# The sink attention's products with v, two token blocks at a time

## The chip, the cores and the metric

The kernel runs on one core of one Trainium2 chip. The metric is the device time of one execution in microseconds (us), as the median of several runs. TensorE is called PE here, VectorE DVE, ScalarE ACT, GpSimd POOL and SyncE SP; PEld is TensorE's loading of weights, which runs beside its products.

## What is computed

The reference is a trunk of two layers (`DEPTH = 2`) over 512 tokens of width 1024. In each layer three token mixers run side by side on the same normalised input: a neighbourhood attention, a sliding-window attention with a sink, and a bidirectional gated DeltaNet. Their outputs are projected, gated and summed; then come an output projection and a gated MLP with a convolution. The change touches the second mixer alone, which has 8 query heads and 2 key/value heads of 64 and works in blocks of 128 tokens. A query block sees its own block of keys and the neighbour on either side:

```python
def sliding_window_gqa(q, k, v, sink):
    ...
    s = jnp.einsum('bnqhgd,bnkhd->bnhgqk', qb, kb).astype(jnp.float32) * (HEAD_DIM ** -0.5)
    ...
    s = jnp.where(valid[None, :, None, None], s, -jnp.inf)
    ...
    p = jax.nn.softmax(jnp.concatenate([s, sink_col], axis=-1), axis=-1)[..., :-1].astype(v.dtype)
    return jnp.einsum('bnhgqk,bnkhd->bnqhgd', p, vb).reshape(B, L, Hq, d)
```

There are four blocks, so the first and the last have two key blocks and the two in the middle three.

## The kernel before

Activations lie with their features on the partitions and all 512 tokens in the free dimension. Every dense product takes 128 x 128 weights and 512 tokens and is made of three PE products (lines 152 to 154: high by high, high by low, low by high part). Weights are loaded by SP's queue (line 140), and split into a high part on ACT (line 142) and a low part on DVE or POOL (line 144).

The source lists the steps of a layer in the order `sp np gg na gp sa gx gz gs gm gc go mn ms mg`: projections, the two attentions (`na`, `sa`), the DeltaNet's parts (`gx`: cross products, `gs`: solve, `gm`: mid, `gc`: scan, `go`: output) and the three merges (`mn`, `ms`, `mg`). That order gives priorities only. A scheduler lays out each engine's stream from all steps at once (`schedule_with_timeline_sim=True`), with times that it plans itself, and packs the buffers in SBUF and PSUM (`auto_bufs=True`); the numbers in `NB` and `CAPS` say how many buffers a name has. Within an engine, instructions then run in the order laid out. `tc.issue_after(x)` puts instructions of a block behind `x` in the stream of x's engine.

`swa_attend` (step `sa`) has two passes (`ep`), each over four token blocks (`b`), each with four heads at a time (two of `e`, two of `gq`). In a block PE makes the scores into banks `at` (lines 529 and 530), DVE adds the mask, scales them and takes the extreme (line 533), ACT takes the exponential (line 541) and scales by the reciprocal sum (line 545). Then for each key block PE transposes the four heads' probabilities into one bank (line 553), and ACT copies it to an SBUF tile `th` (line 555, recorded as line 80, the helper `copy`). Behind the block's last transpose stand the products with v (line 560): each key block gives two products of the source and four PE instructions in the trace, 64 columns of weights wide, for the column halves of the array. They sum into `py`, a bank of `at` that is taken at line 546. ACT writes the high part of `py` to `ysh` (line 564), DVE the low part to `ysl` (line 565). `ms` multiplies both by the branch weights.

`na_attend` (step `na`) has a like inner loop with its products at line 456; it collects the transposed probabilities of two token blocks in a list `pend` and runs the products of both behind the second block's last transpose (line 446).

Of the kernel before, what the change touches and what calls it, by code (L numbers as in the profile page):

```python
# [7 lines left out]
F32 = mybir.dt.float32  # L8
# [3 lines left out]
AF = mybir.ActivationFunctionType  # L12
ALU = mybir.AluOpType
# [34 lines left out]
CAPS = {n + i: c for n, c in (("nqs", 2), ("nkh", 2), ("y", 4), ("ma", 4), ("mg", 8), ("gt", 2), ("W", 2),  # L48
                              ("qd", 2), ("wn", 2), ("vs", 1), ("z", 1), ("act", 22)) for i in "01"}
# [1 line left out]
ORDER = "np na sp sa gg gp gx gs gm gc gz go mn ms mg"  # L51
MERGE = "nsg"
NB = {"mm": 4, "gd": 3, "at": 4, "raw": 3, "hi": 3, "lo": 3}
CAPS |= {}
NB |= {"mm": 6, "gd": 3, "at": 5, "raw": 3, "hi": 3, "lo": 3}
ORDER = "sp np gg na gp sa gx gz gs gm gc go mn ms mg"
MERGE = "nsg"
# [4 lines left out]
def encoder_kernel(ctx, tc, xT, wall, par, cst, nab, out, depth=2, dbg=None):  # L62
    nc = tc.nc
    V, S, T, G = nc.vector, nc.scalar, nc.tensor, nc.gpsimd
# [13 lines left out]
    def copy(name, out, in_, e="S"):  # L78
        if ENG.get(name, e) == "S":
            return S.activation(out=out, in_=in_, func=AF.Copy)  # L80
        return V.tensor_copy(out, in_)
# [3 lines left out]
    def nm(s):  # L85
        cnt[0] += 1
        return f"{s}_{cnt[0]}"
# [4 lines left out]
    def big(dt=F32, shape=(128, 1024), name="u", ln=None):  # L92
        ln = ln or line[0]
        return up.tile(list(shape), dt, tag="u_" + name, name=nm(name), bufs=CAPS.get(name, 1))
# [4 lines left out]
    def tmp(dt=F32, shape=(128, 512), name="t", ln=None):  # L99
        ln = ln or line[0]  # L100
        key = name if name in CAPS else (ln or line[0]) + "_" + name
        return tp.tile(list(shape), dt, tag=key, name=nm(name), bufs=CAPS.get(key, 3))

    def bank(tag, shape=(128, 512)):
        return ps.tile(list(shape), F32, tag=tag, name=nm(tag), bufs=NB[tag])
# [12 lines left out]
    def small(n, name, bufs=3):  # L118
        turn[name, n] = turn.get((name, n), -1) + 1
        return kept(f"{name}{n}_{turn[name, n] % bufs}", n)  # L120
# [165 lines left out]
    for l in range(depth):  # L286
# [224 lines left out]
        def swa_attend():  # L511
            line[0] = "a"

            y["s"] = [None] * 4
            for ep in range(2):
                yh, yl = (big(F32R, (128, 2, 512), name=n) for n in ("ysh", "ysl"))
                for e in range(2):
                    y["s"][2 * ep + e] = (yh[:, e], yl[:, e])
                for b in range(4):
                    kb0, kb1 = max(0, b - 1), min(4, b + 2)  # L520
                    w = 128 * (kb1 - kb0)
                    pr_ = [None] * 4
                    for e in range(2):
                        c0 = 8 * b + 4 * ep + 2 * e
                        mx, sk = small(2, "s", 8), slice(4 * ep + 2 * e, 4 * ep + 2 * e + 2)
                        for gq in range(2):
                            sc = bank("at")
                            q_, kc = qs[2 * ep + e][gq][:, 128 * b:128 * b + 128], slice(128 * kb0, 128 * kb1)
                            T.matmul(sc[:, 0:w], lhsT=q_, rhs=kdh[gq][:, kc], start=True, stop=False)  # L529
                            T.matmul(sc[:, 0:w], lhsT=q_, rhs=kdl[gq][:, kc], start=False, stop=True)  # L530

                            pr = tmp(name="spr")
                            V.tensor_tensor_reduce(out=pr[:, 0:w], in0=sc[:, 0:w], in1=smask[:, 128 * (b == 0):128 * (b == 0) + w], scale=rqs[:, c0 + gq:c0 + gq + 1],
                                                   scalar=nsink[:, sk.start + gq:sk.start + gq + 1], op0=ALU.add, op1=ALU.min, accum_out=mx[:, gq:gq + 1])
                            pr_[2 * gq + e] = pr
                        es, rs = small(2, "s", 8), small(2, "s", 8)
                        V.tensor_tensor(es, mx, P[:, P_SK + sk.start:P_SK + sk.stop], op=ALU.add)
                        S.activation(out=es, in_=es, func=AF.Exp)
                        for gq in range(2):
                            pr = pr_[2 * gq + e]  # L540
                            S.activation(out=pr[:, 0:w], in_=pr[:, 0:w], func=AF.Exp, bias=mx[:, gq:gq + 1], scale=-1.0, accum_out=rs[:, gq:gq + 1])
                        V.tensor_tensor(rs, rs, es, op=ALU.add)
                        V.reciprocal(rs, rs)
                        for gq in range(2):
                            S.activation(out=pr_[2 * gq + e][:, 0:w], in_=pr_[2 * gq + e][:, 0:w], func=AF.Copy, scale=rs[:, gq:gq + 1])
                    py = bank("at")

                    pTs = []
                    for kb in range(kb0, kb1):
                        pt = bank("at")  # L550
                        c0 = 128 * (kb - kb0)
                        for i in range(4):
                            lt = T.transpose(pt[:, 128 * i:128 * i + 128], pr_[i][:, c0:c0 + 128], ident)  # L553
                        pT = tmp(name="th")
                        copy("th", pT, pt)
                        pTs.append(pT)
                    with tc.issue_after(lt.ins):
                        for kb, pT in zip(range(kb0, kb1), pTs):
                            for gq in range(2):
                                T.matmul(py[64 * gq:64 * gq + 64, 0:256], lhsT=vst[:, 128 * kb + 64 * gq:128 * kb + 64 * gq + 64],  # L560
                                         rhs=pT[:, 256 * gq:256 * gq + 256], start=kb == kb0, stop=kb == kb1 - 1, tile_position=(0, 64 * gq))
                    bs = slice(128 * b, 128 * b + 128)
                    pyv = py[:, 0:256].rearrange("p (e t) -> p e t", e=2)
                    S.activation(out=yh[:, :, bs], in_=pyv, func=AF.Copy)
                    V.tensor_tensor(yl[:, :, bs], pyv, yh.bitcast(F32)[:, :, bs], op=ALU.subtract)

        def gdn_gates():
            line[0] = "g"
# [352 lines left out]
        def merge(i, bn):  # L921
# [14 lines left out]
            for m0 in range(0, 8, 2):  # L936
# [6 lines left out]
                for q in range(2):  # L943
# [12 lines left out]
                    elif i == 2:  # L956
# [4 lines left out]
                        mg.append((mh, ml))  # L961

        steps = {"np": na_project, "na": na_attend, "sp": swa_project, "sa": swa_attend, "gg": gdn_gates, "gp": gdn_project,
                 "gx": gdn_cross, "gs": gdn_solve, "gm": gdn_mid, "gc": gdn_scan, "gz": gdn_z, "go": gdn_out}
        for i in ORDER.split():
# [19 lines left out]
        for i in range(NFF):  # L985
            cv = []
            for c in range(2):
# [3 lines left out]
                t = tmp(name="cv", ln=ln)  # L991
# [182 lines left out]
```

## Time and profile before

| | us |
|---|---|
| median of 3 runs | 1661.05 |
| lowest and highest of them | 1659.44 and 1661.3 |
| the profiled execution | 1657.82 |
| its span, first to last instruction | 1656.0 |
| PE busy in the span | 1626.6 |
| DVE, ACT, POOL busy | 1009.8, 767.0, 530.1 |

The profile is of one execution, 3.2 us below the median of the runs. Its span leaves out 1.8 us around the program. Busy time of PE counts the modelled length of its pipelined products, of which the next one starts before the last has ended; how fast PE goes is read from starts that follow each other.

### The profile page before, as it was taken

To read this page: it belongs to the slowest core of one execution; us is meant where nothing else is said; L and a number is where in the kernel's file an instruction comes from. 1 tells how busy PE (TensorE), PEld (TensorE's weight loads), DVE (VectorE), ACT (ScalarE), POOL (GpSimd) and SP (SyncE) were. 2 spreads that over 40 slices of the span, in tenths; PEclk is the share of its full clock that TensorE was granted. 3 is DMA by queue.
4 is the path that set the end of the run, shared out by engine and by line. 5 is a ranking of instruction groups with operands and counts; after the bars stand their busy time and mean duration, and the time that the engine had idled before them with its cause. 6 is when DMAs were issued, how large, how long until landed. Compare 5 with 4: busy or idle time off the path is not lost.

```text
span 1656.0 us, 25095 instructions
## 1 busy us (share of the span) xinstructions
PE 1626.6 (98%) x9196; PEld 1300.2 (79%) x9196; DVE 1009.8 (61%) x1907; ACT 767.0 (46%) x1500; POOL 530.1 (32%) x512
## 2 busy tenths in 40 slices
PE   7999999998999999999999999999999999999999
PEld 5777787676888888878887777876788888888887
DVE  5699895454747777741137998855566577777200
ACT  5556666522444444443335665664234444444321
POOL 0333210130035554554406231102200455455543
PEclk9999999999999999999999999999999999999999
DMA  6222221121532323244333222111225322223442
GB/s 211 87 80 74 86 74 37 33 93 54 184 122 90 99 93 100 95 128 137 125 107 103 80 69 77 52 39 40 89 88 180 115 95 95 99 95 110 134 134 73
DMA packets 91499, 160.45 MB, mean 97 GB/s; under 512 B 10352, under 2 KB 17136, under 8 KB 91376
## 3 DMA queue, kind: packets, MB, share of 16 engines
q1 hardware_dynamic: 91376, 158.85, 29.7%
q8 instruction: 72, 1.18, 0.3%
q14 instruction: 51, 0.42, 0.1%
HBM read 147.80 MB, written 8.39 MB: 94 GB/s over the span
## 4 chain that ended last, share of the span: by engine, by line
PE 85%; DVE 5%; issue 4%; POOL 3%; ACT 2%; DMA 1%; SPq 0%; POOLq 0%; DVEq 0%; ACTq 0%
PE mm L152 24%; PE mm L154 24%; PE mm L153 24%; POOL wl L144 2%; PE at L560 1%; PE at L553 1%; DVE wl L144 1%; PE gd L710 1%; PE at L529 1%; PE at L456 1%; PE gd L843 1%; PE at L530 1%; PE gd L875 1%; PE gd L825 1%; PE gd L346 0%
## 5 line engine op out<-in xcount | busy, mean ns | idle before, releaser
L152 PE MATMUL mm<-hh,wh 128*128 128x512 f32 x1408 | 557.5, 396 | 11.2 <-ACT wh L142 9.9
L154 PE MATMUL mm<-hh,wl 128*128 128x512 f32 x1408 | 555.9, 395 | 5.2 <-DVE wl L144 5.1
L153 PE MATMUL mm<-hl,wh 128*128 128x512 f32 x1408 | 554.9, 395 | 0.5 <-DVE hl L222 0.5
L144 POOL TENSOR_TENSOR wl<-wr,wh 128x512 fp32r<-128x512 f32 (+1 forms) x272 | 363.3, 1347 | 556.7 <-ACT wh L142 545.3
L142 ACT ACTIVATE wh<-wr 128x512 fp32r<-128x512 f32 (+1 forms) x512 | 312.5, 617 | 328.1 <-PE mm L153 222.1
L152 PEld LDWEIGHTS mm<-hh,wh 128*128 128x128 f32 x1408 | 265.9, 189 | 71.5 <-ACT wh L142 12.4
L154 PEld LDWEIGHTS mm<-hh,wl 128*128 128x128 f32 x1408 | 265.9, 189 | 66.0 <-DVE wl L144 9.2
L153 PEld LDWEIGHTS mm<-hl,wh 128*128 128x128 f32 x1408 | 265.8, 189 | 59.0 <-DVE hl L222 3.0
L144 DVE TENSOR_TENSOR wl<-wr,wh 128x512 fp32r<-128x512 f32 x240 | 174.8, 731 | 97.9 <-ACT wh L142 93.5
L245 DVE SCALAR_TENSOR_TENSOR cv<-up,fix,cv 128x511 f32<-128x511 f32 x88 | 143.1, 1626 | 2.8
L154 PE MATMUL mm<-act,wl 128*128 128x512 f32 x352 | 137.1, 390 | 0.6 <-POOL wl L144 0.6
L244 DVE SCALAR_TENSOR_TENSOR cv<-up,fix,cv 128x511 f32<-128x511 f32 x88 | 83.0, 945 | 89.7 <-ACT cv L243 89.7
L152 PE MATMUL mm<-act,wh 128*128 128x512 f32 x352 | 137.1, 389 | 0.3 <-ACT wh L142 0.3
L153 PE MATMUL mm<-act,wh 128*128 128x512 f32 x352 | 137.0, 389 | 0.0
L243 ACT ACTIVATE cv<-up,fix 128x512 f32<-128x512 f32 x88 | 70.8, 809 | 35.5 <-DVE up L291 35.5
L166 ACT ACTIVATE act<-cv 128x512 fp32r<-128x512 f32 x44 | 27.8, 632 | 126.9 <-DVE cv L995 126.9
L154 PEld LDWEIGHTS mm<-act,wl 128*128 128x128 f32 x352 | 66.1, 188 | 15.3 <-POOL wl L144 1.2
L152 PEld LDWEIGHTS mm<-act,wh 128*128 128x128 f32 x352 | 66.1, 188 | 14.2 <-ACT wh L142 0.7
L153 PEld LDWEIGHTS mm<-act,wh 128*128 128x128 f32 x352 | 66.1, 188 | 13.7
L872 POOL TENSOR_TENSOR sd<-SA,fix 64x256 f32<-64x256 f32 x24 | 15.5, 646 | 177.5 <-DVE SA L882 135.5
L1013 DVE TENSOR_TENSOR xo<-xo,mm 128x512 f32<-128x512 f32 x8 | 5.5, 688 | 105.1 <-PE mm L154 105.1
L994 ACT ACTIVATE cv<-cv 128x512 f32<-128x512 f32 x44 | 27.8, 632 | 83.8 <-DVE cv L245 83.8
(292 smaller groups left out, 2153.1 us busy)
## 6 DMA issues: line engine op xcount, KB each, us to landing
wr<-in_wall_dram SPq DMA_DIRECT2D x496, 256.0 KB, 2.8
xs<-xo SPq DMA_DIRECT2D x16, 256.0 KB, 2.2
xo<-xs SPq DMA_DIRECT2D x16, 256.0 KB, 3.9
sw<-raw SPq DMA_DIRECT2D x40, 64.0 KB, 2.0
xf<-in_xT_dram SPq DMA_DIRECT2D x8, 256.0 KB, 6.2
xo<-in_xT_dram SPq DMA_DIRECT2D x8, 256.0 KB, 3.4
xf<-xs SPq DMA_DIRECT2D x8, 256.0 KB, 3.8
wr<-in_wall_dram SPq DMA_DIRECT2D x16, 128.0 KB, 3.1
```

The source lines that it names most:

```text
L142: S.activation(out=hi[:, :n], in_=raw[:, :n], func=AF.Copy)
L144: (G if c >= CH_UP else V).tensor_tensor(lo[:, :n], raw[:, :n], hi.bitcast(F32)[:, :n], op=ALU.subtract)
L152: T.matmul(acc, lhsT=wh, rhs=rh, start=start, stop=False)
L153: T.matmul(acc, lhsT=wh, rhs=rl, start=False, stop=False)
L154: lastm[0] = T.matmul(acc, lhsT=wl, rhs=rh, start=False, stop=stop)
L166: S.activation(out=hi, in_=src, func=AF.Copy)
L243: S.activation(out=dst, in_=src, func=AF.Identity, scale=w[:, 1:2], bias=bias)
L244: V.scalar_tensor_tensor(dst[:, 1:L], src[:, 0:L - 1], w[:, 0:1], dst[:, 1:L], op0=ALU.mult, op1=ALU.add)
L245: V.scalar_tensor_tensor(dst[:, 0:L - 1], src[:, 1:L], w[:, 2:3], dst[:, 0:L - 1], op0=ALU.mult, op1=ALU.add)
L456: T.matmul(py[64 * e:64 * e + 64, 128 * b_:128 * b_ + 128], lhsT=(vt[j][0:wi, b_ + i] if b_ + i < 4 else vt4[0:wi, j])[:, 64 * e:64 * e + 64],
L529: T.matmul(sc[:, 0:w], lhsT=q_, rhs=kdh[gq][:, kc], start=True, stop=False)
L994: S.activation(out=cv[0], in_=cv[0], func=AF.Silu)
```

## The change

In `swa_attend` the list `pend` now lives over the four blocks of a pass. An even block makes its scores, probabilities, transposes and copies as before, puts its key blocks on the list, and goes on. An odd block does the same, then takes the bank `py`, now with a place for either block, and runs the products of both blocks behind its own last transpose. One ACT and one DVE instruction then evict both blocks' columns, 512 instead of 256. The bank is taken behind the transposes instead of ahead of them. `th` in this step gets five buffers where it had three.

```diff
--- before.py
+++ after.py
@@ -51,7 +51,7 @@
 ORDER = "np na sp sa gg gp gx gs gm gc gz go mn ms mg"
 MERGE = "nsg"
 NB = {"mm": 4, "gd": 3, "at": 4, "raw": 3, "hi": 3, "lo": 3}
-CAPS |= {}
+CAPS |= {"a_th": 5}
 NB |= {"mm": 6, "gd": 3, "at": 5, "raw": 3, "hi": 3, "lo": 3}
 ORDER = "sp np gg na gp sa gx gz gs gm gc go mn ms mg"
 MERGE = "nsg"
@@ -516,6 +516,7 @@
                 yh, yl = (big(F32R, (128, 2, 512), name=n) for n in ("ysh", "ysl"))
                 for e in range(2):
                     y["s"][2 * ep + e] = (yh[:, e], yl[:, e])
+                pend = []
                 for b in range(4):
                     kb0, kb1 = max(0, b - 1), min(4, b + 2)
                     w = 128 * (kb1 - kb0)
@@ -543,9 +544,7 @@
                         V.reciprocal(rs, rs)
                         for gq in range(2):
                             S.activation(out=pr_[2 * gq + e][:, 0:w], in_=pr_[2 * gq + e][:, 0:w], func=AF.Copy, scale=rs[:, gq:gq + 1])
-                    py = bank("at")
-
-                    pTs = []
+
                     for kb in range(kb0, kb1):
                         pt = bank("at")
                         c0 = 128 * (kb - kb0)
@@ -553,16 +552,21 @@
                             lt = T.transpose(pt[:, 128 * i:128 * i + 128], pr_[i][:, c0:c0 + 128], ident)
                         pT = tmp(name="th")
                         copy("th", pT, pt)
-                        pTs.append(pT)
+                        pend.append((b, kb, pT, kb == kb0, kb == kb1 - 1))
+                    if b % 2 == 0:
+                        continue
+                    py = bank("at", (128, 2, 2, 128))
                     with tc.issue_after(lt.ins):
-                        for kb, pT in zip(range(kb0, kb1), pTs):
+                        for b_, kb, pT, st, sp_ in pend:
                             for gq in range(2):
-                                T.matmul(py[64 * gq:64 * gq + 64, 0:256], lhsT=vst[:, 128 * kb + 64 * gq:128 * kb + 64 * gq + 64],
-                                         rhs=pT[:, 256 * gq:256 * gq + 256], start=kb == kb0, stop=kb == kb1 - 1, tile_position=(0, 64 * gq))
-                    bs = slice(128 * b, 128 * b + 128)
-                    pyv = py[:, 0:256].rearrange("p (e t) -> p e t", e=2)
-                    S.activation(out=yh[:, :, bs], in_=pyv, func=AF.Copy)
-                    V.tensor_tensor(yl[:, :, bs], pyv, yh.bitcast(F32)[:, :, bs], op=ALU.subtract)
+                                T.matmul(py[64 * gq:64 * gq + 64, b_ % 2], lhsT=vst[:, 128 * kb + 64 * gq:128 * kb + 64 * gq + 64],
+                                         rhs=pT[:, 256 * gq:256 * gq + 256], start=st, stop=sp_, tile_position=(0, 64 * gq))
+                    pend = []
+                    bs = slice(128 * b - 128, 128 * b + 128)
+                    pyv = py.rearrange("p b e t -> p e b t")
+                    S.activation(out=yh[:, :, bs].rearrange("p e (b t) -> p e b t", b=2), in_=pyv, func=AF.Copy)
+                    V.tensor_tensor(yl[:, :, bs].rearrange("p e (b t) -> p e b t", b=2), pyv,
+                                    yh.bitcast(F32)[:, :, bs].rearrange("p e (b t) -> p e b t", b=2), op=ALU.subtract)
 
         def gdn_gates():
             line[0] = "g"
```

## Rows read from the trace of the kernel before

**Rows 1.** The page: busy time of the engines, and the chain that ended last.
```profile
PE 1626.6 (98%) x9196; PEld 1300.2 (79%) x9196; DVE 1009.8 (61%) x1907; ACT 767.0 (46%) x1500; POOL 530.1 (32%) x512
...
PE 85%; DVE 5%; issue 4%; POOL 3%; ACT 2%; DMA 1%; SPq 0%; POOLq 0%; DVEq 0%; ACTq 0%
```

**Rows 2.** Busy us by stretch: PE, PEld, DVE, ACT, POOL; then clock, DMA share, GB/s.
```profile
199.00:326.00 127.00, 125.51 (x1162) 96.73 (x1160) 86.44 (x236) 81.25 (x200) 12.20 (x22) 0.99 0.16 51
...
1017.00:1152.00 135.00, 133.87 (x1216) 101.32 (x1214) 90.08 (x243) 81.96 (x202) 12.49 (x22) 0.99 0.15 48
```

**Rows 3.** PE in order of time (start us, us) at two visits of line 560.
```profile
215.41 0.39 PE L152 MATMUL mm<-hh,wh 128*128 128x512 f32 x1
215.64 0.39 PE L153 MATMUL mm<-hl,wh 128*128 128x512 f32 x1
215.96 0.65 PE L560 MATMUL at<-th,sv 128*64 128x256 f32 x4
216.54 0.44 PE L529 MATMUL at<-kdh,qs 128*128 128x384 f32 x1
...
1036.07 1.08 PE L560 MATMUL at<-th,sv 128*64 128x256 f32 x8
1037.09 0.45 PE L529 MATMUL at<-kdh,qs 128*128 128x384 f32 x1
```

**Rows 4.** Line 560's PE busy time in the eight even blocks' stretches.
```profile
215.00:219.00 4.00, 1.30 (x8) 1.00 0.44 134
...
314.00:318.00 4.00, 1.96 (x12) 1.00 0.10 26
1036.00:1039.00 3.00, 1.08 (x8) 1.00 0.12 46
...
sum 32.00, PE 12.61; mean PE 1.58
```

**Rows 5.** The same in the eight odd blocks' stretches.
```profile
235.00:238.00 3.00, 1.52 (x12) 1.00 0.00 0
...
sum 31.00, PE 11.94; mean PE 1.49
```

**Rows 6.** Groups of instructions (count | busy us, mean ns | idle before).
```profile
L80 ACT ACTIVATE th<-at 128x512 f32<-128x512 f32 x40 | 21.2, 595 | 19.0 <-PE at L553 18.9
...
L565 DVE TENSOR_TENSOR ysl<-at,ysh 128x256 fp32r<-128x256 f32 x16 | 6.7, 420 | 0.7 <-ACT ysh L564 0.6
...
L564 ACT ACTIVATE ysh<-at 128x256 fp32r<-128x256 f32 x16 | 6.1, 380 | 10.7 <-PE at L560 10.7
...
L815 DVE TENSOR_TENSOR kE<-gd,fix 128x512 f32<-128x512 f32 x8 | 5.5, 684 | 0.1
```

**Rows 7.** PE in order of time at a pair of the neighbourhood attention.
```profile
953.96 0.27 PE L446 MATMUL at<-fix,lg 128*120 128x128 f32 x1
954.16 0.81 PE L456 MATMUL at<-pT,nvt 64*64 64x128 f32 x8
...
958.80 0.66 PE L456 MATMUL at<-pT,nvt 128*64 128x128 f32 x8
```

**Rows 8.** ACT at three copies, and PE at a late copy, in order of time.
```profile
296.55 1.57 ACT L80 ACTIVATE th<-at 128x512 f32<-128x512 f32 x3 [1.18 <-PE at L553]
...
1150.10 0.65 PE L560 MATMUL at<-th,sv 128*64 128x256 f32 x4 [0.58 <-ACT th L80]
1150.68 0.68 PE L863 MATMUL gd<-SA,wn 64*64 64x64 f32 x16
```

**Rows 9.** PE in order of time, behind the scan in layer 0.
```profile
388.95 0.66 PE L205 MATMUL gd<-fix,rb 128*128 128x128 f32 x4 [2.61 <-DVE rb L201]
```

**Rows 10.** PE in order of time, then the two stretches of lower clock.
```profile
242.87 3.79 PE L779 MATMUL gd<-WT,Xo 32*32 32x32 f32 x126
...
247.49:250.91 3.41, 3.41 (x10) 0.50 0.30 82
...
1063.28:1066.69 3.41, 3.41 (x9) 0.50 0.23 77
```


## Prediction

> **What bounds the kernel now.** I read the page first, for the share of the engines and the chain that ended last: TensorE (PE) is busy 98% of the span and carries 85% of the chain, the rest being split over engines with 5% or less [rows 1]. Then the table by stretches for the two places where the sink attention runs, one in each layer: of 127.0 us PE is busy 125.5 in the first and of 135.0 us 133.9 in the second, while ScalarE (ACT) and VectorE (DVE) are busy some two thirds [rows 2]. So PE has work at nearly every moment there: dense products, the gated DeltaNet's and the attention's lie mixed in one stream. What the change takes out of ACT or DVE is worth nothing directly; what it takes out of PE's stream moves everything behind it up. What it could gain by ending waits is bounded by PE's idle time in both stretches, (127.0 - 125.5) + (135.0 - 133.9) = 2.6 us.
>
> Then PE's order of time around line 560, the product with v. These products are 64 columns of weights wide, and almost everything around them is 128 wide. I call a run of them with nothing else between a visit. One key block gives four PE instructions. A plain dense product starts 0.23 us after the one before it; the first product of a visit starts 0.32 us after a dense one, a visit of four takes 0.58 us until the next instruction starts, one of eight takes 1.02 us [rows 3]. So four more products inside a visit cost 0.44 us, but a visit of four by itself lengthens PE's stream by 0.32 + 0.58 - 0.23 = 0.67 us. The difference, 0.67 - 0.44 = 0.23 us, is the price of going there and back, whatever is done there.
>
> How many visits there are I read from the same products in sixteen stretches, one for each token block in each of four passes (two ep in two layers). A stretch with eight products is busy 1.08 us if they are one visit and 2 x 0.65 = 1.30 us if they are two; one with twelve is busy 1.96 us in three visits [rows 4]. So each visit shows 0.65 us for its first four products and 0.43 us for every further four. The even blocks (b = 0 and 2) have 80 products, 20 fours, busy 12.61 us in all: 20 x 0.43 = 8.6 us, and (12.61 - 8.6) / 0.22 = 18 visits [rows 4]. The odd blocks have the other 20 fours in 11.94 us: (11.94 - 8.6) / 0.22 = 15 visits, one of them with all twelve products of its block [rows 5]. So there are 33 visits for 16 blocks, because a block's key blocks mostly come apart.
>
> **The change, part by part.**
>
> *Products.* It removes none: 160 stay. It takes away the even block's own place: its products wait for the last transposes of the odd block, some 15 to 20 us later (the first block's run in the stretch from 215, the second's in that from 235 [rows 4, 5]). By then the copies of the even block's two or three key blocks are long made, so they can issue as one visit: 8 first visits for 8 pairs. What comes with them of the odd block is the open quantity. Its key blocks have been transposed just before, and ACT copies them one after another at 0.60 us each [rows 6]; those not ready at that moment make visits of their own. Two bounds and an extreme: none joins, 8 + 15 = 23 visits; the first odd visit always joins, 15; everything joins, 8. The savings against 33 are 10, 18 and 25 visits, at 0.23 us: 2.3, 4.1 and 5.8 us. The nearest rows for the choice are those of the neighbourhood attention, which already runs its products by pairs of blocks: the eight of the even block start right behind the last transposes, those of the odd block 4.6 us later, each a visit of its own [rows 7]. That speaks for the upper count; but there the odd block has one copy step, here two or three, and the first is made while the others are transposed. I take the middle, 19 visits: 14 x 0.23 = 3.2 us saved.
>
> Here a rule can be weighed. The row's 0.23 us per visit stands by itself [rows 3]. The Trainium skill, "TensorEngine Tiling (Array Packing)", Key Properties, says that changing the tiling mode drains TensorE; the trace agrees that there is a price for it, though it names none. Taken with the source's loop, where a block is one run, it would count 16 changes before and 8 after, and the sum would be 8 x 0.23 = 1.8 us; by the visits that the trace shows it is 3.2.
>
> *Evictions.* 16 of 256 columns become 8 of 512: on ACT 16 x 0.380 = 6.1 us become 8 x 0.595 = 4.8, by the copy of 512 columns from PSUM; on DVE 16 x 0.420 = 6.7 become 8 x 0.684 = 5.5, by the nearest row of 512 columns out of PSUM [rows 6]. The 2.5 us are on engines with a third of their time free [rows 2]: nothing. The last eviction before the merge is longer, 0.595 + 0.684 - 0.380 - 0.420 = 0.48 us; PE hides it with merge products that read the other heads' results and with gate products. With no cover it costs 0.48 us at four places, 1.9 us; I take none.
>
> *The bank.* Line 546 takes a PSUM bank for the products ahead of the transposes, in each block; the new code takes one behind the transposes of two blocks. An even block then holds none, and the odd block's scores have a rival fewer for the `at` banks. That can only end waits of PE, so it is between nothing and the 2.6 us of idle time above; I take nothing, since ready dense work fills PE already.
>
> *The transposed probabilities.* Five buffers instead of three, so that five key blocks can be held. No instruction and no DMA more; no queue of SP or POOL is passed.
>
> *What is queued behind the new wait.* The products stand in PE's own order. If the last copy is late when they issue, all PE work behind them waits, the scan's products too. Before, that happened once worth naming: 0.58 us at 1149.5, behind a copy, with the scan's next products queued behind it [rows 8].
>
> Sum against the profiled execution (1657.8 us, span 1656.0): 1657.8 - 3.2 = 1654.6. The median of the runs shown is 3.2 us above that execution, so the forecast for the median is 1661.05 - 3.2 = 1657.8, or 0.2% faster.
>
> **Rivals.**
>
> *All products join.* One visit a pair, 8 in all, and some of PE's idle 2.6 us as well: 5.8 to 8.4 us saved, about 1655 to 1652.6. For it: an even block with eight products and an odd one with twelve already issue in one run [rows 4, 5]. Against: the neighbourhood attention's pairs [rows 7], and that 15 visits for eight odd blocks are nearly two for each.
>
> *It hardly does what it says.* Key blocks of the even blocks go on coming apart, since the scheduler places products by its own planned times and slips dense work between them as it does now; or what is saved at 200 to 330 is lost at PE's waits later in the layer. One such wait of 2.61 us stands at 386, behind the DeltaNet's output norm on DVE, with no other work for PE [rows 9]: if that norm comes no sooner, layer 0 gives back its half. Half of 3.2 stays: 1.6 us, about 1659.5, no change that can be measured. (About 0.2%, 3.3 us, is what can be told from no change.)
>
> *Slower: PE waits for the copies.* If all five key blocks' products are placed right behind the last transposes, PE stands until the odd block's copies are done, up to 1.57 us for three [rows 8]. Eight times that is 12.6 us, less the 5.8 us that single visits save: 6.8 us slower, about 1668. It decides from (5.8 + 3.3) / 8 = 1.1 us a pair. Against: PE carried this wait once in 33 visits, since elsewhere other work was put in between.
>
> *Slower: the clock.* The granted clock fell to 0.50 of full (1.2 of 2.4 GHz) twice, for 3.41 us, the first time right after 126 tiny products of line 779; in those 3.41 us PE had 10 and 9 products where 15 fit at 0.23 us, so a fall costs at least 5 x 0.23 = 1.2 us [rows 10]. If twenty narrow products behind forty transposes did the same, it would be slower by over 0.2% from (3.2 + 3.3) / 1.2 = 5.4, six of the eight pairs; all eight give 9.6 - 3.2 = 6.4 us slower, about 1667. The rows speak against it: the visit of twelve, behind twelve transposes, kept the full clock [rows 5]. In a sentence apart: the Trainium skill, "TensorE: Matmul & The Clock Gate", Part 4, says that a transpose on TensorE does not count as busy for the clock in the same way, which would put longer runs of transposes and narrow products at risk.
>
> *The order elsewhere.* All engines' orders come from one plan over the whole program, and buffers share memory; one edit can move waits far away. Such waits are of 0.5 to 2.6 us each; a handful more or fewer gives 4 us either way.
>
> **How the numbers follow.** Forecast (15 to 23 visits, the rest as it is: 2.3 to 4.1 us saved) 0.50, half of it beyond 3.3 us; all join 0.12; hardly anything 0.12; waiting for copies 0.07; clock 0.03; order elsewhere 0.16 (faster 0.08, same 0.02, slower 0.06). Faster: 0.25 + 0.12 + 0.08 = 0.45. Same: 0.25 + 0.12 + 0.02 = 0.39. Slower: 0.07 + 0.03 + 0.06 = 0.16. The forecast's own range is 1657.0 to 1658.8. The range given is 1652.5, where all join and the idle time goes too, to 1664, where the order elsewhere loses 3 us; some 0.15 lie above (both slow rivals and a tail) and 0.05 below.
>
> **What would show it.** Right: the visits of line 560 fall from 33 to 15 to 23, each pair's first visit has 8 to 16 instructions, 8 evictions of 512 columns take about 0.60 us on ACT and 0.69 on DVE, and PE's idle time in the two stretches stays near 2.6 us. Wrong: visits above 25 (the even block still splits), waits of line 560 on the copies of over 5 us in all, a third fall of the clock, or PE's idle time outside the two stretches changed by more than 3 us, which would mean that the rearranged order and not the visits set the result.

## The result

The changed kernel took 1670.74 us (median of 4 runs, 1668.07 to 1672.57), the kernel before 1660.24 in the runs beside it: 10.5 us slower, a ratio of 1.0069 with a 95% interval of 1.0057 to 1.0081. The forecast was 1657.8, its range ended at 1664.0, and slower had a chance of 0.16. The profiled execution of the changed kernel took 1670.18 us, span 1668.4.

The page of the changed kernel, busy time and chain, for [rows 1]:

```profile
PE 1633.2 (98%) x9196; PEld 1311.4 (79%) x9196; DVE 1007.4 (60%) x1899; ACT 766.4 (46%) x1492; POOL 527.9 (32%) x512
...
PE 87%; DVE 4%; issue 4%; POOL 3%; ACT 1%; DMA 1%; SPq 0%; POOLq 0%; DVEq 0%; ACTq 0%
```

PE has the same 9196 instructions, and yet 6.6 us more busy time; DVE and ACT have 8 fewer each, the merged evictions. PE's idle time in the span went from 29.4 (1656.0 - 1626.6) to 35.2 us (1668.4 - 1633.2).

**What the change was to do, it did.** The changed kernel in order of time, at one pair of blocks (line 562 is the product with v, 560 before; 552 the transpose), for [rows 3]:

```profile
267.34 0.82 PE L552 MATMUL at<-fix,spr 128*128 128x128 f32 x6
268.09 1.52 PE L562 MATMUL at<-th,sv 128*64 128x256 f32 x12
...
271.50 1.08 PE L562 MATMUL at<-th,sv 128*64 128x256 f32 x8
```

The first visit has twelve products, the second eight, and PE waits before neither. By pair, line 562's busy time (stretch, length, busy and count, clock, DMA share, GB/s), for [rows 4, 5]:

```profile
268.00:273.00 5.00, 2.60 (x20) 1.00 0.16 56
290.00:296.00 6.00, 3.04 (x20) 1.00 0.01 3
...
1111.00:1117.00 6.00, 2.82 (x20) 1.00 0.00 0
...
sum 44.00, PE 21.46; mean PE 2.68
```

A pair with two visits shows 2 x 0.65 + 3 x 0.43 = 2.6 us, one with three 2.8, one with four 3.0. The sum gives (21.46 - 40 x 0.43) / 0.22 = 19 visits, 33 before. The groups of the changed kernel, for [rows 6]:

```profile
L562 PE MATMUL at<-th,sv 128*64 128x256 f32 x160 | 21.5, 391 | 0.0
...
L568 DVE TENSOR_TENSOR ysl<-at,ysh 128x512 fp32r<-128x512 f32 x8 | 5.4, 678 | 8.7 <-ACT ysh L567 8.7
...
L567 ACT ACTIVATE ysh<-at 128x512 fp32r<-128x512 f32 x8 | 4.8, 598 | 10.5 <-PE at L562 10.4
```

Line 562 waits for nothing (0.0 us idle before it), and the merged evictions take 598 and 678 ns, where 595 and 684 were forecast.

**Where the time went.** First the stretches of [rows 2] in the changed kernel (PE, PEld, DVE, ACT, POOL busy, then clock, DMA share, GB/s), and two later ones:

```profile
199.00:326.00 127.00, 126.60 (x1107) 98.92 (x1108) 86.63 (x233) 82.56 (x201) 12.06 (x20) 0.99 0.17 54
1017.00:1152.00 135.00, 135.00 (x1146) 105.90 (x1145) 92.57 (x249) 85.53 (x208) 11.68 (x18) 0.97 0.17 54
350.00:400.00 50.00, 43.37 (x388) 34.62 (x387) 21.27 (x46) 10.67 (x18) 7.80 (x9) 0.86 0.19 59
1200.00:1250.00 50.00, 43.75 (x353) 35.18 (x352) 26.00 (x58) 14.08 (x25) 1.58 (x2) 0.93 0.18 57
```

The same two later stretches of the kernel before:

```profile
350.00:400.00 50.00, 47.02 (x372) 37.03 (x369) 22.45 (x46) 13.40 (x23) 7.85 (x6) 1.00 0.22 73
1200.00:1250.00 50.00, 49.41 (x282) 40.31 (x281) 32.19 (x66) 18.79 (x33) 0.00 (x0) 1.00 0.30 99
```

Beside the attention PE now stands idle for 0.4 us instead of 2.6. Behind it, where the DeltaNet's scan ends and its output norm runs, PE stands 6.6 instead of 3.0 us and 6.3 instead of 0.6, and the clock's mean falls from 1.00 to 0.86 and 0.93. What moved is the scan. Its first product of each step (line 863 before, 867 after; 16 instructions a step, 7 steps a layer), in the kernel before:

```profile
306.00:326.00 20.00, 2.04 (x48) 1.00 0.13 41
...
366.00:386.00 20.00, 0.68 (x16) 1.00 0.22 75
```

and in the changed kernel:

```profile
306.00:326.00 20.00, 0.15 (x4) 1.00 0.17 53
...
366.00:386.00 20.00, 2.70 (x48) 0.99 0.24 79
```

Before, three of the seven steps ran by 326, beside the attention's last blocks, and one was left for 366 to 386. Now the attention ends 10 us sooner (its last product starts at 316.1 instead of 325.8), the DeltaNet's middle part 10 us later (its last product at 316.5 instead of 306.0), the scan starts behind both, and three steps are left for the end. In layer 1 the same: the scan's very first product (line 879, 875 before) starts at 1139.8 instead of 1120.6. The end of the scan in the changed kernel, PE in order of time, for [rows 9] (lines 867 and 879: scan; 187, 191 and 205: output norm, lines 908 and 912 its products):

```profile
379.33 0.39 PE L154 MATMUL mm<-hh,wl 128*128 128x512 f32 x1
379.65 0.68 PE L879 MATMUL gd<-VN,kT 64*64 64x64 f32 x16
381.42 1.13 PE L867 MATMUL gd<-SA,wn 64*64 64x64 f32 x16 [1.09 <-DVE SA L884]
383.06 1.13 PE L879 MATMUL gd<-VN,kT 64*64 64x64 f32 x16 [0.51 <-DVE VN L870]
384.77 1.15 PE L867 MATMUL gd<-SA,wn 64*64 64x64 f32 x16 [0.58 <-DVE SA L884]
...
387.14 0.43 PE L908 MATMUL gd<-qd,SA 128*64 128x64 f32 x4
387.35 0.43 PE L912 MATMUL gd<-Q,VN 128*64 128x64 f32 x4
...
391.03 0.66 PE L187 MATMUL gd<-sq,fix 128*32 128x128 f32 x8 [0.70 <-ACT sq L914]
392.09 0.48 PE L191 MATMUL gd<-fix,sb 128*128 128x128 f32 x1 [0.40 <-ACT sb L80]
395.00 1.08 PE L205 MATMUL gd<-fix,rb 128*128 128x128 f32 x4 [2.43 <-DVE rb L201]
...
399.55 0.50 PE L152 MATMUL mm<-y,wh 128*128 128x512 f32 x1
```

At 379.33 stands the last dense product and at 399.55 the next one; between them PE has only a chain through DVE and ACT, and waits at nearly every link. This stretch without a dense product takes 20.2 us, and 17.3 in layer 1 (from 1208.99). In the kernel before, the longest ones behind the attention are 5.6 us (from 386.0) and 2.8 (from 1208.3). And the clock falls, for [rows 10]:

```profile
385.75:399.41 13.66, 9.60 (x145) 8.10 (x142) 4.91 (x15) 1.50 (x3) 0.00 (x0) 0.50 0.01 2
1215.19:1218.61 3.42, 2.93 (x58) 2.74 (x53) 0.00 (x0) 0.45 (x1) 0.00 (x0) 0.50 0.00 0
1222.02:1225.43 3.41, 3.01 (x42) 2.71 (x44) 1.44 (x3) 0.63 (x1) 0.00 (x0) 0.50 0.02 5
```

1.2 of 2.4 GHz for 20.5 us in the two tails, where the kernel before had none. Elsewhere this trace has three falls, 13.7 us in all (3.4 from 105.9, 3.4 from 245.8, 6.8 from 1068.4), the kernel before the two of [rows 10], 6.8 us. Last, each layer from the attention's first score product to the first dense product of the last merge (columns as above), before:

```profile
199.20:428.60 229.40, 223.65 (x1809) 174.03 (x1808) 143.25 (x344) 113.79 (x255) 29.19 (x36) 0.99 0.21 66
1016.60:1248.30 231.70, 229.84 (x1834) 178.55 (x1833) 146.78 (x349) 113.99 (x258) 28.23 (x34) 0.99 0.20 66
```

and after:

```profile
200.10:434.30 234.20, 227.00 (x1810) 179.06 (x1808) 143.03 (x341) 113.63 (x252) 28.37 (x36) 0.96 0.20 65
1022.10:1260.70 238.60, 232.35 (x1833) 183.69 (x1832) 145.25 (x345) 113.43 (x254) 28.68 (x34) 0.97 0.21 66
```

These two stretches are longer by 4.8 and 6.9 us, 11.7 of the 12.4 us between the spans. The first starts 0.9 us later; up to there PE's order is the same in both kernels, and two executions of one kernel (runs 1 and 11 below) differ there by 0.8 us, so this need not be the change. By the medians the loss is 10.5 us, and the visits gave 3.0 back, so the new order cost 13.5, some 14 us.

### The profile page after: what moved, and what is told of

Its sections match the earlier page's. It is cut to its first block, busy times and chain, and to the rows that moved or that the text cites. A ratio compares the mean times of both kernels' runs of the same rounds, so it can differ in the third digit from the quotient of the medians.

```text
span 1668.4 us, 25075 instructions
## 1 busy us (share of the span) xinstructions
PE 1633.2 (98%) x9196; PEld 1311.4 (79%) x9196; DVE 1007.4 (60%) x1899; ACT 766.4 (46%) x1492; POOL 527.9 (32%) x512
## 4 chain that ended last, share of the span: by engine, by line
PE 87%; DVE 4%; issue 4%; POOL 3%; ACT 1%; DMA 1%; SPq 0%; POOLq 0%; DVEq 0%; ACTq 0%
PE mm L152 25%; PE mm L154 25%; PE mm L153 25%; POOL wl L144 2%; PE at L552 1%; PE at L562 1%; PE gd L714 1%; PE at L530 1%; DVE wl L144 1%; PE gd L847 1%; PE at L456 1%; PE gd L829 1%; PE at L531 1%; PE gd L867 0%; PE gd L879 0%
## 5 line engine op out<-in xcount | busy, mean ns | idle before, releaser
L153 PEld LDWEIGHTS mm<-act,wh 128*128 128x128 f32 x352 | 66.1, 188 | 13.7
L291 DVE TENSOR_TENSOR up<-mm,rstd 128x512 f32<-128x512 f32 x88 | 59.5, 680 | 9.7 <-ACT rstd L239 9.7
```

The costliest lines, as they stand in the source:

```text
L153: T.matmul(acc, lhsT=wh, rhs=rl, start=False, stop=False)
L291: V.tensor_tensor(dst, acc, rstd, op=ALU.mult)
```

## The experiments

Theory A: the loss is the order. The scan loses its place beside the attention, the dense products are used up between its steps, and its end and the output norm run bare, that is with no other work for PE, which stands idle and at half clock. Theory B: the pairs themselves cost, by later products and evictions and waits for the copies. Theory C: the clock falls by narrow products behind long runs of transposes in the attention. "As built" in the expectations means PE's order of instructions, where the dense products issued so far serve as a measure of place: 1104 (layer 0) and 4128 (layer 1) are all that don't need the output norm.

**1. Pairs, with the attention behind the scan in the list of priorities.**

```diff
-ORDER = "sp np gg na gp sa gx gz gs gm gc go mn ms mg"
+ORDER = "sp np gg na gp gx gz gs gm gc sa go mn ms mg"
```

> The changed kernel with one name moved in the planner's priority list: the sink attention stands behind the DeltaNet's scan instead of ahead of its convolution; all of the computation is kept. In the order as built the paired products stay (18 visits, 19 in the changed kernel), the scan stands within the dense work again and the output norm ends 24 and 12 dense products before the dense work is used up. Theory A (the loss is the order: the scan and the output norm end with nothing beside them): the granted clock of 0.50 in the scan's tail goes, TensorE's idle time falls back to some 18 us, and the time is at or below the kernel before, 1653 to 1660. Theory B (the paired products themselves cost: later products and evictions, waits for the copies): the pairs are all there, so the time stays at 1667 to 1673. Theory C (the clock falls by narrow products behind runs of transposes in the attention): as B, 1667 to 1673, with the same stretches at 0.50.

Measured: 1641.74 us against 1659.05, ratio 0.9894 (0.9881 to 0.9908). B and C fall: every pair is there, in 18 visits, and the loss is gone. A had the direction and missed the size: its range began at 1653, and the gain over the kernel before is 17.3 us. The scan's line 867 in this kernel:

```profile
286.00:306.00 20.00, 0.88 (x22) 1.00 0.09 27
306.00:326.00 20.00, 1.85 (x48) 1.00 0.18 57
```

It starts ahead of 306 and has made 64 of its 112 products by 326 (six lie across 306 and count in both rows), 48 in the kernel before. The stretches from first score to last merge:

```profile
199.20:418.20 219.00, 217.41 (x1810) 172.91 (x1808) 143.26 (x341) 114.64 (x252) 28.38 (x36) 1.00 0.22 69
1006.50:1230.10 223.60, 222.28 (x1833) 178.27 (x1831) 146.54 (x344) 113.84 (x254) 27.30 (x34) 0.99 0.22 70
```

10.4 and 8.1 us shorter than before. Of these 18.5 us, 4.7 are PE's idle time (5.8 + 1.9 before, 1.6 + 1.3 here); 15 visits fewer are 15 x 0.23 = 3.4. The other 10 are busy time of the same instructions in another order. The traces show a part of it: in these stretches PE's stream leaves its 128x128 tiles for narrower ones 101 times in the kernel before and 72 times here. At a visit's price of 0.23 us that is an estimate of 6.7 us, the 3.4 of the visits included. Some 7 us stay open, one fall of the clock fewer (3.4 us at 0.50) among them.

**2. Single products, with the same list.** The kernel before with the same edit of the list.

> The kernel before (products of each block by themselves) with the same name moved behind the scan in the priority list; all of the computation is kept. As built it has 24 visits of the products (33 before), and the scan and the output norm both stand far inside the dense work. Theory A: 1652 to 1660, so that the pairs are worth 1 us or less once the scan is covered in both. Theory B: the kernel with single products is the faster one of the two with the list changed, by some 8 us or more. Theory C: as A for this kernel by itself.

Measured: 1651.38 us, ratio 0.9957 (0.9945 to 0.997). So the list alone gives 7.7 us, and with it the pairs are worth 9.6 us, not 1 us or less as A said, nor a loss as B said. The 6 visits between 24 and 18 are 1.4 us of that. Part of the rest is the loss from the other side. With single products all of the scan stands beside the attention's last blocks, and there the dense products are too few; in layer 1:

```profile
1129.00:1150.00 21.00, 16.11 (x200) 11.61 (x198) 12.16 (x39) 10.52 (x29) 4.04 (x6) 0.92 0.04 14
```

In these 21 us there are 6 dense products among 200, PE stands 4.9 us, behind the scan's chain and the attention's, and the clock's mean is 0.92. Over both stretches PE stands 8.2 us here (3.1 and 5.1) and 2.9 in the run above.

**3. A control: the attention moved only ahead of the middle part.**

```diff
+ORDER = "sp np gg na gp gx gz gs sa gm gc go mn ms mg"
```

> The changed kernel with the sink attention moved in the priority list ahead of the DeltaNet's middle part alone, behind its sums and gates; all of the computation is kept. As built the visits are 18, but the scan still ends and the output norm still runs with no dense work left (as in the changed kernel). Theory A: moving the name does nothing by itself, the tail is bare as before: 1667 to 1673, with the granted clock of 0.50 in the tail. Theory B and C: the same, 1667 to 1673; what this run tells apart is A from the reading that any move of the name in the list gives the time back, which expects 1660 or less.

Measured: 1666.10 us, ratio 1.0044 (1.003 to 1.0057), 0.9 us below what was expected. The clock is at 0.50 from 381.7 to 388.5 and again from 391.9, and in layer 1 from 1204.3 and 1214.5, as in the changed kernel. The reading that any move of the name gives the time back falls: with the tail still bare, the kernel stays 7.1 us above the kernel before, where the changed one was 10.5 above it, and run 1 is 17.3 below.

**4. Pairs, with fewer PSUM banks in the planner's bound for the attentions.**

```diff
-NB |= {"mm": 6, "gd": 3, "at": 5, "raw": 3, "hi": 3, "lo": 3}
+NB |= {"mm": 6, "gd": 3, "at": 3, "raw": 3, "hi": 3, "lo": 3}
```

> The changed kernel with three instead of five PSUM banks in the planner's bound for the attention's scores, transposes and products; the priority list as it was, all of the computation kept. As built the attention is spread wider, the visits are 15, and the scan and the output norm stand inside the dense work (the scan ends at 900 of 1104 dense products in layer 0 and 3973 of 4128 in layer 1). Theory A: the tail is covered, no clock of 0.50 there, 1650 to 1660. Theory B: pairs with fewer banks wait longer for the copies, 1670 or more. Theory C: fewer visits behind transposes, but as many narrow products: 1667 to 1673.

Measured: 1690.95 us, ratio 1.019 (1.0176 to 1.0204): A's number missed by 31 us, and B's "1670 or more" came out. The output norm was covered on the chip, with the clock at 1.00 from 1186.2 on. But the bound also holds for the neighbourhood attention, which I hadn't weighed, and for the scores; PE in this kernel, in order of time:

```profile
212.95 0.30 PE L445 MATMUL at<-fix,lg 128*128 128x128 f32 x1 [1.97 <-DVE lg L442]
...
225.45 0.39 PE L530 MATMUL at<-kdh,qs 128*128 128x256 f32 x1 [3.53 <-DVE fix L534]
```

The first score comes at 215.7 and 1049.1 instead of 200.1 and 1022.1. From there to the last merge it takes 222.0 and 231.9 us, 12 and 7 less than in the changed kernel; but part of the work has moved ahead of that point (1761 products in the stretch instead of 1810), and in layer 1 the attention's own end runs bare, with the clock at 0.50 from 1169.1 to 1186.2. So this run doesn't tell A and B apart.

**5. Single products, scan held behind the attention.** In the kernel before, the scan's first products wait in PE's order for the last product of line 560.

```diff
+                                lastv[0] = T.matmul(py[64 * gq:64 * gq + 64, 0:256], lhsT=vst[:, 128 * kb + 64 * gq:128 * kb + 64 * gq + 64],
...
+                            with behind(None if s else lastv[0]):
+                                T.matmul(pd[r, hh], lhsT=kT(ns[d], hh)[r], rhs=VN(ns[d])[r, hh], start=True, stop=True,
...
```

> The kernel before, attention and its products untouched; only the first products of each layer's DeltaNet scan are held behind the last product of the sink attention, so that the scan can't start beside the attention. All of the computation is kept. As built it has 32 visits (33 before), the scan ends and the output norm runs with no dense work left, as in the changed kernel. Theory A (the loss is the place of the scan): most of the changed kernel's loss without any pair, and the 14 visits are not saved either: 1666 to 1675, with the granted clock at 0.50 in the tail of the scan. Theory B (the pairs cost): 1657 to 1661, as before.

Measured: 1678.77 us against 1657.46, ratio 1.0128 (1.0113 to 1.0144). Without one pair, the late scan costs 21 us, and the time is 4 us above the upper end of what A expected. Its line 863:

```profile
306.00:326.00 20.00, 0.00 (x0) 1.00 0.13 40
...
386.00:406.00 20.00, 1.56 (x16) 0.59 0.01 2
```

No step runs before 326, and the clock's mean is 0.59 in the 20 us from 386. The two stretches grew by 8.6 and 11.8 us. The place of the scan alone makes more than the changed kernel's whole loss.

**6. Pairs, tail filled.** In the changed kernel, 48 products of constants a layer that nothing reads; the tail's own work is unchanged.

```diff
+    def fill(n, m):
+        acc = bank("gd")
+        with behind(m):
+            for k in range(2 * n):
+                lastf[0] = T.matmul(acc[:, 0:256], lhsT=blk, rhs=frt[:, 0:256], start=True, stop=True)
+        return lastf[0]
...
+                    if s > 5:
+                        fill(3, lv)
...
+        if pad:
+            fill(10, m)
```

> The changed kernel with work added that nothing reads: 128x256 products of constants, 6 behind each of the last three groups of the scan's products and 6, 4 and 20 in the output norm's first chain, in the tails where TensorE has nothing else (48 in each layer). The order of the rest is the changed kernel's. If the tails' loss is partly the clock that falls to 0.50 there, the added work keeps it at 1.00 and the products of the output norm and what follows run at full speed, so that the time falls by some 3 to 8 us although work is added: 1662 to 1668. If the clock is not the matter (the stalls alone are, or the pairs), the added 48 products lengthen the chains or change nothing: 1670 to 1676.

Measured: 1666.56 us, ratio 1.0055 (1.0043 to 1.0068). That interval overlaps the changed kernel's, measured on another chip, so it was run again beside it (9 and 10). In this execution the clock was at 1.00 in the tails but for 3.4 us from 383.4.

**7. One part alone: single products, merged evictions.**

```diff
-                    py = bank("at")
+                    if b % 2 == 0:
+                        py = bank("at", (128, 2, 2, 128))
...
+                    if b % 2 == 0:
+                        continue
```

> One part of the change alone: the products of each block run by themselves as before, but into one bank of two blocks, and both blocks are evicted together. All of the computation is kept. As built there are 29 visits; in layer 0 the scan ends and the output norm runs with no dense work left, in layer 1 the scan ends 48 dense products before the end of the dense work and the output norm ends with it. Theory A: a loss in layer 0 alone, of some 5 us, and 4 visits fewer: 1661 to 1666. Theory B, the later eviction costs by itself in both layers: 1666 to 1672; the products' place is what costs: 1657 to 1661.

Measured: 1660.78 us against 1657.46, ratio 1.0016 (1.0007 to 1.0025). B's later evictions as the cause of 10 us fall. A's 5 us in layer 0 missed as well: the stretches grew by 0.4 and 0.9 us, with the clock at 0.50 for 6.8 us from 389.0 and 3.4 from 1211.6. A bare output norm alone, with the scan covered up to its last step, costs little, since the kernel before stood there for 2.6 us too [rows 9].

**8. Pairs, attention between middle part and scan.**

```diff
+ORDER = "sp np gg na gp gx gz gs gm sa gc go mn ms mg"
```

> The changed kernel with the sink attention in the priority list between the DeltaNet's middle part and its scan (behind the scan in the faster version); all of the computation is kept. As built 17 visits, the scan ends 72 and 48 dense products before the dense work is used up, the output norm ends just with it. Theory A: no bare tail, hence no clock of 0.50 there, 1641 to 1652. Theory B and C: 1667 to 1673 by the pairs.

Measured: 1647.52 us, ratio 0.9936 (0.9923 to 0.9948), as A expected in its time. Its clock part missed: the clock was at 0.50 for 3.4 us from 383.2 and for 6.8 us from 1199.0, at the output norm, which ends with the dense work. Its time lies between the changed kernel's and run 1's, as its scan does (from 294.5 in layer 0; 289.8 in run 1, 316.4 in the changed kernel).

**9 to 11. Three kernels once more, on one chip.**

> The changed kernel once more, unaltered, so that it stands on one chip beside the next two: 1667 to 1673, 9 to 12 us over the kernel before.

> The changed kernel with 48 unread products in each layer's bare tail, once more, on one chip with the changed kernel. If the clock in the tails is a part of the loss, 2 to 6 us under the changed kernel; if not, the same or above it.

> The pairs with the sink attention behind the scan in the priority list, once more, on one chip with the changed kernel: 1640 to 1644, some 29 us under the changed kernel and some 17 under the kernel before.

Measured: the changed kernel 1670.35 us (1668.67 to 1670.48), filled 1666.60 (1664.76 to 1668.72), pairs with the attention behind the scan 1642.10 (1641.24 to 1643.18), the kernel before 1659.01; ratios 1.0066, 1.0045 and 0.9899. The filled kernel's group of the added work, and of the output norm's products:

```profile
L188 PE MATMUL gd<-frt 128*128 128x256 f32 x96 | 14.3, 294 | 0.0
...
L927 PE MATMUL gd<-qd,SA 128*64 128x64 f32 x128 | 7.9, 225 | 0.0
```

The same group in the changed kernel:

```profile
L908 PE MATMUL gd<-qd,SA 128*64 128x64 f32 x128 | 13.0, 303 | 0.0
```

14.3 us of PE work that nothing reads made the kernel 3.75 us faster by the medians; the runs of one kernel lie 2 to 4 us apart, so the size is rough. In 380 to 400 and 1200 to 1220 the clock is 1.00 with it, 0.66 and 0.91 without (first trace of the changed kernel); the output norm's products start 0.12 us apart instead of 0.21. What this owes to the clock is read from the stretches without a dense product. In layer 0, first the changed kernel of run 9:

```profile
379.52 0.39 PE L154 MATMUL mm<-hh,wl 128*128 128x512 f32 x1
...
399.08 0.80 PE L152 MATMUL mm<-y,wh 128*128 128x512 f32 x1
```

and the filled one of run 10:

```profile
378.90 0.39 PE L154 MATMUL mm<-hh,wl 128*128 128x512 f32 x1
...
395.49 0.73 PE L152 MATMUL mm<-y,wh 128*128 128x512 f32 x2
```

19.6 us became 16.6, and in layer 1 17.4 became 14.9. Between these products PE's order is the same but for the added work, which by itself can only delay the rest, so some 5.5 us of the loss are the clock's in this pair of executions. Behind them part of the dense products comes in another order in the filled kernel, and at the end its lead is 3.8 us (spans of 1668.6 and 1664.8).

## Why the prediction was wrong

*What bounds the kernel.* PE does, as read. The step that failed is the sentence built on it, that what leaves PE's stream "moves everything behind it up". The stream isn't kept: the same edit gave another one, with the scan 10 and 19 us later, and a chain through other engines cost PE next to nothing here only where dense products stood beside it.

*Products.* Right: 33 visits became 19, the middle of the bounds, and line 562's group is 21.5 us where 560's was 24.5: 3.0 us saved, 3.2 forecast. (The odd blocks' stretches stand 10 to 20 us behind the even ones' in the kernel before [rows 4, 5], not 15 to 20; no term of the sum rests on it.)

*Evictions.* Right, 598 and 678 ns, and nothing on PE waits for them; run 7 puts them, with the order that came with them, at 3.3 us together (1.2 to 4.1 by the interval).

*Bank and buffers.* PE's idle time beside the attention fell from 2.6 to 0.4 us, inside the bound given. Neither was run by itself: with five `th` buffers alone, or with the bank taken behind the transposes alone, the kernel before as built keeps PE's instructions in the order that it had.

*Waiting for copies.* This rival fell: 0.0 us before line 562.

*The clock.* Its mechanism fell. In the eight stretches of pairs the granted clock is 1.00, the first visits behind runs of transposes among them. The third fall that was set down as a sign did show, but elsewhere: above all in the tails, on the scan's chain of narrow products with waits of 0.5 to 1.1 us between them. Beside the attention it fell at the tiny products of line 783 (779 before), at 245.8 and 1068.4, as in the kernel before [rows 10]. The Trainium skill, "TensorE: Matmul & The Clock Gate", "Loop structure matters more than you think", shows a wait for DMA as what makes TensorE cold, and an eviction from PSUM as harmless where the next matmuls follow at once. The trace agrees with the condition and widens the example: the waits ahead of the fall at 385.75 are for DVE and not for a DMA, and what follows them at once is only the chain's own next products, sixteen narrow ones at a time.

*The order elsewhere.* This is the rival that came true, at a price over three times too small and with 0.06 for its slow side. It was sized by waits "of 0.5 to 2.6 us each; a handful more or fewer", 4 us; it was some 14 us, because a chain that is moved out of its cover loses at every link, and the clock with it. The place was named under another rival, the wait at 386 behind the output norm, "if that norm comes no sooner" [rows 9]; what I didn't ask is what hid the scan ahead of it. The sign set down for this case showed: PE's idle time outside the two stretches rose by 8.0 us (5.8 in the span, and 2.2 less inside), where 3 was the mark.

What stays open: why the planner put the middle part 10 us later once the products came in pairs, and some 7 of the 10 us of busy time that run 1 saves beyond visits and idle time.

## What to carry to other kernels

Where one scheduler lays out all engines from priorities, price an edit in two parts: what it takes from the stream, and which long chain the new order leaves without other work. The first was right here to 0.2 us, the second was over four times as large. When a local saving comes out as a loss, move the chain's place before undoing the edit: the same pairs with one name moved in the list are 17 us faster than the kernel before.

## What was not expected of the hardware

Work added to an idle TensorE shortened the kernel: 96 products of 128x256, 14.3 us busy, for 3.75 us less time, with the granted clock at 1.00 where it had been 0.50 for up to 13.7 us in one piece (3.4 and 6.8 us, 3.4 apart, in the same place of run 9). One fall can be priced there: runs 6 and 10 are the same kernel, run 6 was at 0.50 for 3.4 us from 383.4, and its stretch without a dense product took 17.9 us instead of 16.6.
